# Strassen block products in part of a down projection, a triangular inverse moved to GpSimd, norm sums in three pieces

## The chip, the cores and the metric

The kernel runs on one core of a Trainium2 chip. The metric is the device time of one execution in microseconds (us). Engines are named as in the profile: PE is TensorE's matmul stream, DVE VectorE, ACT ScalarE, POOL GpSimd, SP SyncE, which only issues DMAs here.

## What is computed

One layer of a hybrid decoder on 512 prompt tokens and 8 decode tokens, 520 in all, in fp32, with D = 1024 and a hidden width of 2816:

```python
def swiglu(x, w_gate, w_up, w_down):
    return (jax.nn.silu(x @ w_gate) * (x @ w_up)) @ w_down
...
x = x + 0.5 * rmsnorm(swiglu(rmsnorm(x, ffn1_pre_g), ...), ffn1_post_g)
m, ... = token_mixer(rmsnorm(x, mix_pre_g), ...)
x = x + rmsnorm(m, mix_post_g)
x = x + 0.5 * rmsnorm(swiglu(rmsnorm(x, ffn2_pre_g), ...), ffn2_post_g)
```

The mixer projects with `w_in`, runs four heads of retention (with rope) and four heads of gated DeltaNet side by side, gates and merges both branches and projects with `w_out`. The chunked DeltaNet solves a unit lower triangular system for every chunk of tokens:

```python
a_mat = jnp.eye(c) + jnp.where(strict, bc[..., :, None] * dm * kk, 0.0)
u_v = lax.linalg.triangular_solve(a_mat, bc[..., None] * vc, left_side=True, lower=True, unit_diagonal=True)
```

## The kernel before

**Products.** Features lie on the 128 partitions, tokens along the free axis in two halves of HC = 260. An fp32 product is made of three passes on split operands (`passes`, L294 to L296): high weight by high x, high weight by low x, low weight by high x. One *step* is a contraction tile of 128 for both halves, that is 6 matmuls of 128x260. Weights are split on the chip: ACT copies the high part (L254), DVE subtracts for the low part (`wlo`, L255).

**Stages.** FFN1's gate and up projections run to 245 us of the profiled span, its down projection from there to 378, the mixer to about 870, FFN2's gate and up to 1115 and its down projection to 1247; the last norm and the output follow. Most gate/up tiles are already made by Strassen's scheme: a pair of tiles as seven block products (`seven`, table `SEVEN`) that collect in seven PSUM banks (`sv`), whose weight blocks (L273, 128x512) are summed by adding DMAs and by DVE.

**Down** (L487 to L518) makes 8 output tiles one after another; each has 22 steps over the hidden tiles, in weight units of 8, 7 and 7 contraction tiles. Hidden tiles (`h`) are split into `hh` (ACT, L606) and `hl` (DVE, L608): the first 10 (`SPLIT_H`) while gate/up still runs, the other 12 by the generator `late` when down has begun. When tile 2 begins, the next x is loaded by 8 DMAs of 260 KB.

**Order.** Everything is issued in program order, one in-order queue for each engine. `product`, `seven` and `staged` call `tick()` after each step; side work (hidden tiles, norms, mixer heads) is written as generators that give a number of ticks at each `yield` and are continued when the clock of ticks gets there. So a row on DVE or POOL stands where its tick stands, and a row that waits holds all behind it on its engine. Weights are loaded by SP into two raw buffers (`RAW_BUFS`), split into nine slots (`SPLIT_BUFS`) and looked two units ahead; a pool of 68 slots (`big`) holds x, h, operands and results.

**The inverse** (`inverse`, L1251) of a DeltaNet head: the diagonal blocks of 32 rows are inverted by forward substitution, 31 columns with a multiply (L1279) and a subtract (L1280) each over 128 partitions = 16 blocks by 8 groups of result columns, 4 columns a group. Heads 0 and 2 run on POOL, heads 1 and 3 on DVE. The result goes through DRAM (`s2`, one write of 64 KB at L1283, four reads at L1286) and a transpose on DVE (L1293); then larger blocks are put together on PE (`pV` at L1303 is the first).

**Norm sums.** `sums` (L356, `ss`) adds the squares of 65 tokens at a time over partitions by a matmul with one column, 4 pieces a half (`PIECES`, `PW`); `root` takes the power on POOL (L351, `rs`); `spread` (L362, `rb`) spreads it over the partitions by one matmul a piece.

Of the kernel before, what the change touches and what calls it, by code (L numbers as in the profile page):

```python
# [15 lines left out]
P = 128  # L16
# [15 lines left out]
PIECES, PW = 4, HC // 4  # L32
# [8 lines left out]
SPLIT_H = 10  # L41
# [19 lines left out]
def units():  # L61

    out = []
    for f in (1, 2):
# [4 lines left out]
        for d in range(KD):  # L69
            out += [(f"dn{f}", d, 0, 8), (f"dn{f}", d, 8, 15), (f"dn{f}", d, 15, 22)]  # L70
# [15 lines left out]

SEVEN = ((0, "B11", 0), (2, "T3", 1), (0, "T2", 3), (2, "T4", 4), (1, "B21", 5), (0, "T1", 6), (0, "B22", 9))


def stream(first):  # L90

    at = []
    for m in range(first, KF):
        for i, (_, _, place) in enumerate(SEVEN):
            if m == KF - 1 and i == 4:
                place = 6.5
            at.append((7 * m + place, m, i))
    return [(m, i) for _, m, i in sorted(at)]


class Kernel:
    def __init__(self, ctx, tc, a):
# [14 lines left out]
        for u in self.unit_list:  # L117
            if u[0] != "seven":
# [3 lines left out]
            if u[1:3] not in pairs:  # L122
                g += 1
                pairs[u[1:3]] = g
            self.group.append(pairs[u[1:3]])
# [13 lines left out]
        self.tasks = []  # L139
        self.hold = False  # L140
# [4 lines left out]
    def spawn(self, gen):  # L145
        self.tasks.append([self.now, gen])

    def tick(self):
# [3 lines left out]
        for t in list(self.tasks):  # L152
            if t[0] <= self.now:
                try:
                    t[0] = self.now + (next(t[1]) or 1)
# [32 lines left out]
    def load_to(self, j):  # L188

        nc, a = self.nc, self.a  # L190
        while self.raw_next < min(self.group[min(j, len(self.unit_list))] + RAW_BUFS, self.group[-1]):
            u = self.unit_list[self.first_of[self.raw_next]]
            if u[0] == "seven":
# [10 lines left out]
                t = [t[:, 0:KH], s3, None, a22, t[:, KH:KD], s1, None]  # L204
            else:
# [11 lines left out]
    def cost(self, j):  # L217
        return 1 if self.unit_list[j][0] == "seven" else 2

    def prefetch(self, force=False, most=9):  # L220
# [5 lines left out]
        while self.split_next < min(last, len(self.unit_list)):  # L226
            j = self.split_next
            seven = self.cost(j) == 1
            if seven and self.hold_sums and not force:
                break  # L230
            if j >= self.use_next + (8 if seven and self.ahead else self.ahead) or self.slots_used + self.cost(j) > free:
                break
            if seven:
# [23 lines left out]
    def split_seven(self, j):  # L257
# [16 lines left out]
        if i == 4:  # L274
            t[s4] = self.slot("s4", (P, KH, P))
            nc.vector.tensor_tensor(t[s4], t[4], t[s2], ALU.subtract)

# [76 lines left out]
    def sums(self, ps, acc, n):  # L354
        for c in range(n):
            self.nc.tensor.matmul(ps[0:PW, c : c + 1], acc[:, c * PW : (c + 1) * PW], self.ones[:, 0:1], start=True, stop=True)  # L356

    def spread(self, r):

        pb = self.bank("rb")  # L360
        for c in range(PIECES):
            self.nc.tensor.matmul(  # L362
                pb[:, c * PW : (c + 1) * PW], r[0:PW, c : c + 1].to_broadcast([PW, P]), self.ident[0:PW, 0:PW], start=True, stop=True
# [41 lines left out]
    def pre_rms(self, xs, r, plus):  # L405
# [3 lines left out]
        for hf in range(2):  # L409
            for k in range(KD):  # L410
                while len(xs[hf]) <= k:
                    yield 1
# [3 lines left out]
        while not self.leads:  # L416
            yield 1
# [68 lines left out]
    def down(self, xin, pieces, gpost, gnext, held, plus=None, plus_next=None, x_from=None):  # L486
# [4 lines left out]
        xs, r = [[], []], [None, None]  # L491

        def evac(d, hf, ps):
            if len(y) <= d:
                y.append(self.slot("y"))
            c0, n = HALVES[hf]
            self.square_sum(acc[hf], ps, hf, d == 0, nc.vector)
# [11 lines left out]
        for d in range(KD - held):  # L509
            if d == 2 and x_from is not None:  # L510
                self.x = [self.slot("x") for _ in range(KD)]
                for k in range(KD):
                    nc.sync.dma_start(out=self.x[k], in_=x_from[:, k, :])
            ps = self.product(job(), xin, "dn")
            for hf in range(2):
                evac(d, hf, ps[hf])
        self.staged([job] * held, sum(pieces), xin, "dn", lambda j, hf, ps: evac(KD - held + j, hf, ps), False)
# [33 lines left out]
    def token_factors(self, xs, gcol, F):  # L551

        nc = self.nc
        while len(xs[1]) < KD or not self.rooted:
            yield 1
# [24 lines left out]

    def seven(self, F, name, banks, i):

        b, tokens, _ = SEVEN[i]
# [12 lines left out]
    def ffn(self, plain, xs, r, gpre, gpost, gnext, plus, plus_next, x_from):  # L596
        nc = self.nc
        tt = nc.vector.tensor_tensor
        hx = [[], []]
        hs = []  # L600
        F = {x: [] for x in ("B11", "B21", "B22", "T1", "T2", "T3", "T4")}

        def split_h(h):
# [5 lines left out]
            for hf, (c0, n) in enumerate(HALVES):  # L609
                hx[hf].append((hh[:, c0 : c0 + n], hl[:, c0 : c0 + n]))  # L610

        def hidden(pg, pu):

            h = self.slot("h")
            while r[0] is None or r[1] is None:
                yield 1
# [10 lines left out]
            yield 2  # L627
            yield from split_h(h)

        def pair(m):  # L630
# [39 lines left out]
            def second(t):  # L670
# [5 lines left out]
                if m < SPLIT_H:  # L676
                    yield 1
                    yield from split_h(h)
                else:
                    hs.append(h)  # L680
# [6 lines left out]
        def leads():  # L687
            for j in range(0, len(lead), 2):
                yield from hidden(*lead[j : j + 2])
# [946 lines left out]
```

## Time and profile before

| | |
|---|---|
| median of 3 runs | 1265.9 us (1264.64 to 1267.73) |
| profiled execution | 1265.27 us |
| span in its trace | 1263.5 us |
| PE busy | 1214.7 us (96%) |
| DVE busy | 864.6 us (68%) |
| ACT busy | 538.5 us (43%) |
| POOL busy | 255.9 us (20%) |
| HBM traffic | 131 GB/s over the span |

The shares are means over stages that differ. In the two down stages DVE is busy for less than a third of the time; in gate/up and in parts of the mixer for eight to nine tenths. The table of waits says after which instruction PE went on, and the windows of the trace say for a stretch how busy each engine was and which share of its full clock TensorE was granted.

### The profile page before, as it was taken

Reading aid. Unit: us, or ns where it says so; the run is one execution under the profiler, and the core shown is the slowest. Engines: PE = TensorE matmul, PEld = TensorE weight load, DVE = VectorE, ACT = ScalarE, POOL = GpSimd, SP = SyncE. Lnnn points to the kernel's source line nnn. Section 1 sums busy time; section 2 is a strip of 40 time slices with the busy share of each in tenths; the row PEclk is TensorE's granted clock in tenths of the full one; section 3 lists DMA queues with packets and bytes.
Section 4 is the critical chain, followed back from the end, with each engine's and each line's share of the span. In section 5 each row is a group of like instructions: output and inputs, shape, how many; then the busy total and the mean of one; then the engine's idle time right before and its main releaser. Section 6 shows DMA issues by size and latency. Waiting matters only on the chain.

```text
span 1263.5 us, 25461 instructions
## 1 busy us (share of the span) xinstructions
PE 1214.7 (96%) x10073; PEld 1203.5 (95%) x10073; DVE 864.6 (68%) x1911; ACT 538.5 (43%) x1117; POOL 255.9 (20%) x378
## 2 busy tenths in 40 slices
PE   8999999999999998899999999999989999999995
PEld 7999999999999998899999999999989999999995
DVE  8888888653347887878786766547878878852224
ACT  6566555432234654213334333334645655542210
POOL 4111112000023257136401112204211111100003
PEclk8999999999999899999999999999989999999997
DMA  5677777353332233232434554322377777524321
GB/s 176 178 185 193 184 180 176 94 157 92 91 94 68 87 101 112 77 95 85 129 123 123 197 179 151 118 84 84 122 201 180 178 178 184 144 78 160 92 76 68
DMA packets 76552, 166.60 MB, mean 132 GB/s; under 512 B 14481, under 2 KB 19953, under 8 KB 76433
## 3 DMA queue, kind: packets, MB, share of 16 engines
q1 hardware_dynamic: 64144, 140.69, 34.9%
q0 software_dynamic: 12288, 24.29, 11.3%
q8 instruction: 79, 1.29, 0.4%
q14 instruction: 41, 0.33, 0.1%
HBM read 155.24 MB, written 9.70 MB: 131 GB/s over the span
## 4 chain that ended last, share of the span: by engine, by line
PE 72%; DVE 13%; DMA 4%; issue 3%; ACT 3%; POOL 3%; SPq 0%; DVEq 0%; ACTq 0%; POOLq 0%
PE sv L294 9%; PE sv L295 9%; PE sv L296 9%; PE dn L295 7%; PE dn L294 7%; PE dn L296 7%; PE p L294 5%; PE p L295 5%; PE p L296 5%; DMA s<-gu_in 3%; DVE wlo L255 2%; PE br L294 1%; PE br L295 1%; PE br L296 1%; DVE cv L1049 1%
## 5 line engine op out<-in xcount | busy, mean ns | idle before, releaser
L294 PE MATMUL p<-xhl,whi 128*128 128x260 f32 x784 | 234.5, 299 | 0.0
L295 PE MATMUL p<-xhl,whi 128*128 128x260 f32 x784 | 224.8, 287 | 0.0
L296 PE MATMUL p<-xhl,wlo 128*128 128x260 f32 x784 | 224.4, 286 | 0.0
L295 PE MATMUL dn<-hl,whi 128*128 128x260 f32 x704 | 200.1, 284 | 2.7 <-DVE hl L608 2.7
L294 PE MATMUL dn<-hh,whi 128*128 128x260 f32 x704 | 200.1, 284 | 0.4 <-ACT hh L606 0.4
L296 PE MATMUL dn<-hh,wlo 128*128 128x260 f32 x704 | 199.5, 283 | 0.0
L255 DVE TENSOR_TENSOR wlo<-raw,whi 128x1024 fp32r<-128x1024 f32 (+2 forms) x133 | 156.8, 1192 | 56.9 <-ACT whi L254 56.7
L294 PE MATMUL sv<-th,w 128*128 128x260 f32 x592 | 169.0, 285 | 3.4 <-ACT u L640 3.2
L296 PE MATMUL sv<-th,w 128*128 128x260 f32 x592 | 168.3, 284 | 0.0
L295 PE MATMUL sv<-tl,w 128*128 128x260 f32 x592 | 168.1, 284 | 0.0
L254 ACT CAST whi<-raw 128x1024 fp32r<-128x1024 f32 (+2 forms) x133 | 128.1, 979 | 59.3 <-DMA raw<-dn_in 52.0
L294 PEld LDWEIGHTS p<-xhl,whi 128*128 128x128 f32 x784 | 151.4, 193 | 0.7
L295 PEld LDWEIGHTS p<-xhl,whi 128*128 128x128 f32 x784 | 151.6, 193 | 0.1
L296 PEld LDWEIGHTS p<-xhl,wlo 128*128 128x128 f32 x784 | 151.1, 193 | 0.0
L273 DVE TENSOR_TENSOR w<-s,w 128x512 fp32r<-128x512 f32 x148 | 101.4, 689 | 52.7 <-ACT w L272 51.0
L295 PEld LDWEIGHTS dn<-hl,whi 128*128 128x128 f32 x704 | 133.3, 189 | 3.3 <-DVE hl L608 3.3
L294 PEld LDWEIGHTS dn<-hh,whi 128*128 128x128 f32 x704 | 133.2, 189 | 0.6 <-ACT hh L606 0.6
L296 PEld LDWEIGHTS dn<-hh,wlo 128*128 128x128 f32 x704 | 133.5, 190 | 0.0
L294 PE MATMUL sv<-xhl,w 128*128 128x260 f32 x444 | 126.2, 284 | 5.2 <-DVE t L619 4.6
L215 POOL DMA_DIRECT2D s<-gu_in x74 | 65.0, 977 | 320.1 <-DMA s<-gu_in 152.0
L295 PE MATMUL sv<-xhl,w 128*128 128x260 f32 x444 | 125.7, 283 | 0.0
L296 PE MATMUL sv<-xhl,w 128*128 128x260 f32 x444 | 125.4, 282 | 0.0
(364 smaller groups left out, 2891.6 us busy)
## 6 DMA issues: line engine op xcount, KB each, us to landing
raw<-gu_in SPq DMA_DIRECT2D x50, 512.0 KB, 4.6
raw<-win_in SPq DMA_DIRECT2D x49, 512.0 KB, 3.6
s<-gu_in SPq DMA_DIRECT2D x74, 256.0 KB, 5.3
s<-gu_in POOLq DMA_DIRECT2D x74, 256.0 KB, 4.9
raw<-dn_in SPq DMA_DIRECT2D x32, 448.0 KB, 3.4
a<-gu_in SPq DMA_DIRECT2D x37, 256.0 KB, 5.5
raw<-dn_in SPq DMA_DIRECT2D x16, 512.0 KB, 3.5
x<-x SPq DMA_DIRECT2D x16, 260.0 KB, 5.4
```

Source lines behind the costliest of these rows:

```text
L215: self.nc.gpsimd.dma_start(out=out, in_=term, accum_op=ALU.add)
L254: self.nc.scalar.copy(hi[:, ks], t[:, ks])
L255: self.nc.vector.tensor_tensor(lo[:, ks], t[:, ks], hi[:, ks].bitcast(F32), ALU.subtract)
L273: nc.vector.tensor_tensor(w[:, 1], t[i], w[:, 0].bitcast(F32), ALU.subtract)
L294: mm(ps, hi[:, k, :], xh, start=first, stop=False, skip_group_check=more)
L295: mm(ps, hi[:, k, :], xl, start=False, stop=False, skip_group_check=more)
L296: mm(ps, lo[:, k, :], xh, start=False, stop=last, skip_group_check=more)
L1049: nc.vector.scalar_tensor_tensor(out=acc, in0=cin[:, j : j + SEQ], scalar=w[:, j : j + 1], in1=acc, op0=ALU.mult, op1=ALU.add)
```

## The change

**Down.** Tile 0 and tile 7 stay plain products, with their units in the order 8..14, 15..21, 0..7. Tiles 1 to 6 are made in pairs, three in each FFN. For a pair, contraction tiles 8 to 21 are 14 plain steps for each tile (`rest`); the other 8 are a 2x2 block product (two output tiles by two token halves, contraction in two halves of four tiles), made by seven block products of 4 contraction tiles, 12 matmuls each, of sums of weight blocks and of h blocks. The seven go to six banks, four of which already hold the plain part.

```diff
+DOWN7 = ((0, "B11"), (2, "B21"), (4, "T4"), (0, "N"), (1, "T3"), (0, "T1"), (3, "B22"))
...
-            out += [(f"dn{f}", d, 0, 8), (f"dn{f}", d, 8, 15), (f"dn{f}", d, 15, 22)]
+            rest = [(f"dn{f}", d, 8, 15), (f"dn{f}", d, 15, 22)]
+            if d in (0, KD - 1):
+                out += rest + [(f"dn{f}", d, 0, 8)]
+            else:
+                out += rest
+                if d % 2 == 0:
+                    out += [("down7", f, d - 1, i) for i in range(7)]
...
+    def split_down7(self, j):
+        ...
+        a11, a12, a21, a22 = self.loaded[self.group[j]]
+        if i == 3:
+            tt(a22, a21, a22, ALU.add)
+            tt(a21, a21, a11, ALU.add)
+            tt(a11, a11, a22, ALU.add)
+            tt(a12, a12, a11, ALU.add)
+        src = (a11, a12, a22, a11, a21, a22, a12)[i]
+        w = self.whl.tile([P, 2, KH, P], F32R, tag="w", name=self.name("w7"))
+        ...
+        self.nc.scalar.copy(w[:, 0], src)
+        tt(w[:, 1], src, w[:, 0].bitcast(F32), ALU.subtract)
```

A pair's blocks use two raw loads of 512 KB, both raw buffers, until the last of the seven is split. The results come together on DVE from copies that ACT makes of banks that are used again:

```diff
+    def down_pair(self, rest, F, done, load_x):
+        ...
+        for z in range(2):
+            banks += self.product([(self.next_unit(), range(7)), (self.next_unit(), range(7, 14))], rest, "dn")
+        ...
+        for i in range(7):
+            self.product7(DOWN7, F, "dn", banks, i)
+            if i == 0:
+                v["p"] = self.work("u", HC)
+                nc.scalar.copy(v["p"], banks[a])
+            elif i == 1:
+                add(0, 0, v["p"], banks[r11])
+            elif i == 3:
+                v["u"] = self.work("u", HC)
+                nc.scalar.copy(v["u"], banks[a])
+                if load_x:
+                    load_x()
+            elif i == 4:
+                v["qs"] = self.work("q", HC)
+                nc.scalar.copy(v["qs"], banks[q])
+                v["qu"] = self.work("c", HC)
+                tt(v["qu"], banks[q], v["u"], ALU.subtract)
+                add(1, 0, v["qu"], banks[r21])
+            ...
```

`add` is one DVE addition and then the square, its sum and y, as before. The loads of x move from tile 2 into the third pair, behind its fourth block.

**Hidden tiles.** `SPLIT_H = (8, 21)`: tiles 8 to 20 are split while gate/up runs; tile 21 and tiles 0 to 7 by a generator when down has begun. The latter gives 16 halves of 260 columns and, for four pairs of tiles, four DVE sums of 260 and two splits of 520:

```diff
+        def down_operands():
+            ...
+            for k in range(KD):
+                for hf, (c0, n) in enumerate(HALVES):
+                    first8[hf].append(parts(late[k][:, c0 : c0 + n], "hp"))
+                yield 2
+            for k in range(KH):
+                ...
+                tt(ta[:, 1], x12, x22, ALU.subtract)
+                tt(tb[:, 0], ta[:, 1], x11, ALU.subtract)
+                tt(tb[:, 1], x21, tb[:, 0], ALU.add)
+                tt(ta[:, 0], x11, x12, ALU.subtract)
+                yield 1
+                for t, names in ((tb, ("N", "T4")), (ta, ("T1", "T3"))):
+                    hi, lo = self.slot("th", (P, 2, HC), F32R), self.slot("tl", (P, 2, HC), F32R)
+                    nc.scalar.copy(hi, t)
+                    tt(lo, t, hi.bitcast(F32), ALU.subtract)
```

DVE where the first down tile's results are taken (`y`): before, between the last of the late `hl` and the splits of the next weights:

```order
L608 TENSOR_TENSOR hl_3673<-h_3215,hh_3672 128x520
L608 TENSOR_TENSOR hl_3683<-h_3351,hh_3682 128x520
L498 TENSOR_SCALAR y_3692<-dn_3500,gh 128x260
L498 TENSOR_SCALAR y_3692<-dn_3501,gh 128x260
L255 TENSOR_TENSOR wlo_3698<-raw_3498,whi_3697 128x896
L255 TENSOR_TENSOR wlo_3712<-raw_3576,whi_3711 128x1024
L255 TENSOR_TENSOR wlo_3766<-raw_3701,whi_3765 128x896
```

and now, with the parts of tiles 0 to 7 (`hp`) and the first operand sums (`ta`, `tb`, `tl`) ahead of them:

```order
L840 TENSOR_TENSOR hp_3680<-h_1305,hp_3680 128x260
L840 TENSOR_TENSOR hp_3683<-h_1305,hp_3683 128x260
L861 TENSOR_TENSOR ta_3698<-h_411,h_873 128x260
L862 TENSOR_TENSOR tb_3699<-ta_3698,h_411 128x260
L863 TENSOR_TENSOR tb_3699<-h_873,tb_3699 128x260
L864 TENSOR_TENSOR ta_3698<-h_411 128x260
L869 TENSOR_TENSOR tl_3711<-tb_3699,th_3710 128x520
L608 TENSOR_SCALAR y_3714<-dn_3508,gh 128x260
L608 TENSOR_SCALAR y_3714<-dn_3509,gh 128x260
L302 TENSOR_TENSOR wlo_3720<-raw_3506,whi_3719 128x896
L302 TENSOR_TENSOR wlo_3736<-raw_3582,whi_3735 128x896
```

The first tile's results and the next weights (`wlo`) now stand behind the operand work on DVE.

**Inverse.** All four heads substitute on POOL. The 8 groups now hold columns g, g+8, g+16 and g+24, so that column j touches only the first j//8 + 1 of the four, and the result is written by 8 DMAs:

```diff
-        yield from self.inverse(AT, out, nc.vector if h % 2 else nc.gpsimd)
+        yield from self.inverse(AT, out, nc.gpsimd)
...
-            n = 31 - j
+            n, nq = 31 - j, j // 8 + 1
...
-        nc.sync.dma_start(out=s2.rearrange("b c (g q) i -> (b c g) (q i)", q=4), in_=T.rearrange("p q i -> p (q i)"))
+        columns = s2.rearrange("b c (q g) i -> g (b c) q i", q=4)
+        for g in range(8):
+            nc.sync.dma_start(out=columns[g], in_=T[g:P:8])
```

DVE before, in the substitution of head 1 (`pack` is its work tile, `rp` and `u` are retention's rope, `gdr` the decode norm):

```order
L1279 TENSOR_TENSOR pack_6347<-L_6343,pack_6347 128x4x28
L1280 TENSOR_TENSOR pack_6347<-pack_6347 128x4x28
L1379 COPY gdr_6535<-cb_6587 128x64
L1065 TENSOR_TENSOR rp_6590<-p_6515,cos_5395 128x260
L1066 TENSOR_TENSOR u_6591<-p_6515,sin_5396 64x260
L1067 TENSOR_TENSOR u_6591<-p_6515,sin_5396 64x260
L1068 TENSOR_TENSOR rp_6590<-rp_6590,u_6591 128x260
L1065 TENSOR_TENSOR rp_6590<-p_6516,cos_5395 128x260
```

POOL now, at the same head (L1438 and L1439 are the two lines of the substitution, `rdec` a copy of rope's result for decode):

```order
L1438 TENSOR_TENSOR pack_6488<-L_6484,pack_6488 128x28
L1439 TENSOR_TENSOR pack_6488<-pack_6488 128x28
L1227 COPY rdec<-rp_6738 128x8
L1438 TENSOR_TENSOR pack_6488<-L_6484,pack_6488 128x27
L1439 TENSOR_TENSOR pack_6488<-pack_6488 128x27
L1438 TENSOR_TENSOR pack_6488<-L_6484,pack_6488 128x26
```

The two rows a column have left the queue that carries rope and stand on POOL around a copy that needs rope's result.

SP before, at the end of head 1's substitution, whose result is `pack_6347`:

```order
L1415 DMA sd_7149<-sgdn_in 128x512
L208 DMA raw_7173<-win_in 128x1024
L1283 DMA s_1166_7210<-pack_6347 128x128
L1286 DMA pack_6347<-s_1166_7210 32x4x32 x4
L1415 DMA sd_7256<-sgdn_in 128x512
```

and now, where it is `pack_6488`:

```order
L1576 DMA sd_7297<-sgdn_in 128x512
L251 DMA raw_7321<-win_in 128x1024
L1444 DMA s_1235_7358<-pack_6488 64x1x32 x8
L1447 DMA pack_6488<-s_1235_7358 32x4x32 x4
L1576 DMA sd_7411<-sgdn_in 128x512
```

One write has become eight between a load of decode state or weights (`sd`, `raw`) and the next.

**Norm sums.** `PIECES` goes from 4 to 3 and `PW` from 65 to 87 (three of 87 cover 260 tokens with one taken twice); the power works on 87x6 and 87x3 in place of 65x8 and 65x4.

The other edits (`LATER`, which is empty, the count of spawned generators, `yield 0`) move no instruction.

Over the whole program PE has 9208 matmuls and transposes in place of 9280, of which down has 72 fewer. DVE has 30 instructions more, ACT 86, POOL 124 and SP 28.

## Rows read from the trace of the kernel before

**Rows 1.** Page: busy us (share of the span) and instructions of each engine

```profile
PE 1214.7 (96%) x10073; PEld 1203.5 (95%) x10073; DVE 864.6 (68%) x1911; ACT 538.5 (43%) x1117; POOL 255.9 (20%) x378
```

**Rows 2.** PE's waits by line and releaser: us total, times, longest

```profile
PE sv L294 <- DVE t L619: 4.6, 1, 4.6
...
PE cs L1371 <- DVE gsq L1483: 3.2, 1, 3.2
...
PE dn L295 <- DVE hl L608: 2.7, 3, 1.3
...
PE po L1110 <- DVE st L1118: 2.0, 1, 2.0
PE pV L1303 <- DVE pack L1279: 1.5, 1, 1.5
...
PE ks L1214 <- DVE S L1230: 1.3, 1, 1.3
```

**Rows 3.** Windows: busy us (instructions) by engine, granted clock, DMA share, GB/s

```profile
64.00:96.00 32.00, 32.00 (x271) 32.00 (x270) 28.67 (x56) 20.25 (x43) 5.21 (x6) 1.00 0.76 191
274.00:366.00 92.00, 92.00 (x768) 92.00 (x768) 27.66 (x41) 19.86 (x29) 0.00 (x0) 1.00 0.37 114
...
480.00:512.00 32.00, 28.00 (x219) 27.36 (x217) 26.26 (x74) 10.22 (x28) 21.32 (x48) 0.95 0.35 97
640.00:672.00 32.00, 32.00 (x276) 31.45 (x275) 27.96 (x106) 10.56 (x25) 3.45 (x6) 0.95 0.30 103
1118.00:1130.00 12.00, 10.27 (x71) 9.87 (x71) 9.37 (x14) 8.62 (x16) 0.00 (x0) 0.86 0.46 145
```

**Rows 4.** VectorE's groups by line: busy us, mean ns, idle before, releaser

```profile
L255 DVE TENSOR_TENSOR wlo<-raw,whi 128x1024 fp32r<-128x1024 f32 (+2 forms) x133 | 156.8, 1192 | 56.9 <-ACT whi L254 56.7
L273 DVE TENSOR_TENSOR w<-s,w 128x512 fp32r<-128x512 f32 x148 | 101.4, 689 | 52.7 <-ACT w L272 51.0
...
L608 DVE TENSOR_TENSOR hl<-h,hh 128x520 fp32r<-128x520 f32 x44 | 28.8, 695 | 1.5 <-ACT hh L606 1.5
...
L668 DVE TENSOR_TENSOR h<-c,s 128x260 f32<-128x260 f32 x37 | 15.7, 423 | 0.0
```

**Rows 5.** Groups by line, 458 to 672 us: VectorE, then GpSimd

```profile
L1280 DVE TENSOR_TENSOR pack<-pack 128x124 f32<-128x124 f32 (+30 forms) x62 | 16.0, 258 | 2.1
L1279 DVE TENSOR_TENSOR pack<-L,pack 128x124 f32<-128x124 f32 (+30 forms) x62 | 13.6, 219 | 0.8
...
L1280 POOL TENSOR_TENSOR pack<-pack 128x124 f32<-128x124 f32 (+30 forms) x62 | 23.9, 386 | 4.9
L1279 POOL TENSOR_TENSOR pack<-L,pack 128x124 f32<-128x124 f32 (+30 forms) x62 | 22.8, 368 | 4.0 <-DMA L<-s 0.8
L1069 POOL COPY rdec<-rp 128x8 f32<-128x8 f32 x8 | 8.0, 1005 | 32.0 <-DVE rp L1068 27.7 <-PE sT L1093 4.3
```

**Rows 6.** Line L1279 by engine: ns min/median/max, first and last start us

```profile
L1279 POOL TENSOR_TENSOR pack<-L,pack x62: 196/302/1235, 458.6 to 615.2; 128x124 f32<-128x124 f32 x2, 128x120 f32<-128x120 f32 x2, 128x116 f32<-128x116 f32 x2, 128x112 f32<-128x112 f32 x2
L1279 DVE TENSOR_TENSOR pack<-L,pack x62: 134/218/285, 500.8 to 671.0; 128x124 f32<-128x124 f32 x2, 128x120 f32<-128x120 f32 x2, 128x116 f32<-128x116 f32 x2, 128x112 f32<-128x112 f32 x2
```

**Rows 7.** VectorE in order of time, 627.5 to 630 us: start, us

```profile
628.57 0.28 DVE L1279 TENSOR_TENSOR pack<-L,pack 128x124 f32<-128x124 f32 x1
```

**Rows 8.** GpSimd's groups by shape; PE at a norm: start, us, idle

```profile
L1151 POOL TENSOR_TENSOR rr<-se,mhalf 128x8 f32<-128x8 f32 x4 | 8.5, 2132 | 5.1 <-DVE cin L1038 5.1
...
L351 POOL TENSOR_TENSOR rs<-ms,mhalf 65x8 f32<-65x8 f32 x3 | 6.5, 2162 | 25.1 <-DVE ms L347 25.1
...
378.76 0.63 PE L356 MATMUL ss<-ones,acc 128*65 128x1 f32 x8 [0.92 <-DVE acc L395]
...
382.84 1.10 PE L362 MATMUL rb<-cst,rs 65*128 65x65 f32 x8 [1.19 <-POOL rs L351]
```

**Rows 9.** DMA issues by group: KB each, median us from issue to landing

```profile
x<-x SPq DMA_DIRECT2D x16, 260.0 KB, 5.4
...
s<-pack SPq DMA_DIRECT2D x4, 64.0 KB, 3.2
```

More of the change, by code (lines that the diff above doesn't have):

```diff
@@ L31 @@
 HALVES = ((0, HC), (HC, HC))
-PIECES, PW = 4, HC // 4
+PIECES, PW = 3, -(-HC // 3)
+PIECE_AT = [i * (HC - PW) // (PIECES - 1) for i in range(PIECES)]
 KH = KD // 2
@@ L117, in __init__ @@
         for u in self.unit_list:
-            if u[0] != "seven":
+            if u[0] not in ("seven", "down7"):
                 g += 1
@@ L154, in tick @@
                 try:
-                    t[0] = self.now + (next(t[1]) or 1)
+                    steps = next(t[1])
+                    if steps:
+                        t[3] += 1
+                        steps += t[2].get(t[3], 0)
+                    t[0] = self.now + max(steps, 1)
                 except StopIteration:
@@ L204, in load_to @@
                 t = [t[:, 0:KH], s3, None, a22, t[:, KH:KD], s1, None]
+            elif u[0] == "down7":
+                t = []
+                for d in (u[2], u[2] + 1):
+                    raw = self.raw.tile([P, KD, P], F32, tag="raw", name=self.name("raw"))
+                    nc.sync.dma_start(out=raw, in_=a[f"dn{u[1]}"][d, :, 0:KD, :])
+                    t += [raw[:, 0:KH], raw[:, KH:KD]]
             else:
@@ L688, in leads @@
             for j in range(0, len(lead), 2):
-                yield from hidden(*lead[j : j + 2])
+                yield from hidden(j // 2, *lead[j : j + 2])
         self.spawn(leads())
@@ L701, in ffn @@
             if n == 3:
-                self.spawn(hidden(pg, pu))
+                self.spawn(hidden(plain - 1, pg, pu))
             if m not in pairs:
@@ L705, in ffn, with parts @@
             banks, at = pairs[m]
-            self.seven(F, "sv", banks, i)
+            self.product7(SEVEN, F, "sv", banks, i)
             at(i)
-        def late():
-            while len(hx[1]) < SPLIT_H or len(hs) < KF - SPLIT_H:
-                yield 1
-            for h in hs:
-                yield from split_h(h)
-                yield 1
-        self.spawn(late())
-        return self.down(hx, (8, 7, 7), gpost, gnext, 1, plus, plus_next, x_from)
+        def parts(src, name):
+            t = self.slot(name, (P, 2, HC), F32R)
+            nc.scalar.copy(t[:, 0], src)
+            tt(t[:, 1], src, t[:, 0].bitcast(F32), ALU.subtract)
+            return t[:, 0], t[:, 1]
@@ L720, in run @@
+        self.spawn(down_operands())
+        return self.down(first8, (8, 7, 7), gpost, gnext, 1, plus, plus_next, x_from, (rest, first8, D))
     def run(self):
```

162 lines of the change are left out of this document (117 added, 45 removed).

## The prediction

> **What bounds the kernel now.** I read the busy times first: PE is busy 1214.7 of 1263.5 us, DVE 864.6, POOL 255.9 [rows 1]. PE is the bound, so only two things can shorten the span: less work for PE, and fewer moments in which PE stands still or runs slowly. The table of PE's waits says after whom it stood still [rows 2], and the windows say where another engine is close to full [rows 3]. In the middle of the first down stage PE is busy 92.00 of 92 us with 768 matmuls while DVE is busy 27.66 [rows 3]: there nothing but PE counts, and a matmul of 260 columns costs 92.00/768 = 0.120 us. In the mixer it is otherwise: between 480 and 512 us PE is busy 28.00 of 32, DVE 26.26, POOL 21.32, and the granted clock is 0.95 [rows 3]. The long waits there end with a DVE instruction (`cs` 3.2, `po` 2.0, `pV` 1.5, `ks` 1.3 us, together 8.0 [rows 2]): DVE's queue is in the way. All sums below start from the profiled execution, 1265.3 us (span 1263.5 plus 1.8 around it); the median of the runs is 0.6 us higher.
>
> **Down: PE's share.** A pair's first 8 contraction tiles cost 8 steps x 6 matmuls x 2 tiles = 96 matmuls; seven blocks of 12 cost 84. Six pairs save 6 x 12 = 72 matmuls, 72 x 0.120 = **8.6 us**, all on the path because PE never waits there [rows 3]. The seven use the same 260 columns, so no price by matmul changes.
>
> **Down: what it adds on DVE.** A pair has 4 block sums and 7 splits of 512 columns where two splits of 1024 stood: 11 x 0.69 - 2 x 1.19 = +5.2 us, and six more operations of 260 columns, 6 x 0.42 = +2.5 us [rows 4]. A pair takes PE (168 + 84) x 0.120 = 30 us, and DVE is now busy about 0.30 of such a stretch [rows 3], so it goes from 9 to some 17 us of 30. That is covered. The tight place is the start. From the end of gate/up PE has 22 steps of tile 0, 28 of the first pair and three blocks before the first block that needs in-place sums: 50 x 0.72 + 3 x 1.44 = 40 us. DVE owes until then one `hl` (0.70), 16 parts of 260 (6.8), 16 operand sums (6.8), 8 splits of 520 (5.6), six weight splits (7), two results (1) and 8 operations of 512 (5.5): 33 us of 40. So it fits in sum, but each split stands behind the ACT copy that it subtracts and behind the queue shown in the first piece of order. The last `hl` now has 14 plain steps (10 us) of cover, which had none in the kernel before; against that, tile 0's third unit needs the eight pairs of parts at 0.85 us a step when PE eats 0.72, a lag of 8 x 0.13 = 1 us at most if they start on time. In before the same place cost 2.7 us of waits over both stages [rows 2] and, in the second, a window at clock 0.86, that is 0.14 x 12 = 1.7 us [rows 3]. I take new waits of 1 to 2 us at each start, equal to what they replace: **0**, with -4 (none left) and +6 (3 us more at each start) as ends. Later pairs need two raw loads, both buffers, before the next unit's load can go; those units are used 20 us of PE later. The third pair's x load sets 8 x 260 KB ahead of tile 7's last unit on SP; a load of x lands 5.4 us after its issue in the middle of its burst [rows 9]. I take **+0.5**, with 0 and +3.
>
> **Hidden tiles.** Thirteen instead of ten are split within gate/up. There DVE is at 28.67 of 32 with PE at 32.00 where such splits already stand [rows 3], so they are free. At the start of FFN2's stream, where PE waits 4.6 us for one DVE result [rows 2], the first hidden tiles' splits go from the queue ahead of it, about one 0.70 us operation [rows 4]: **-0.6**, with 0 and -2.
>
> **Substitution.** DVE loses 62 pairs of operations, 16.0 + 13.6 = 29.6 us [rows 5], from the very queue that ends PE's waits. POOL takes them. Its operation costs 0.38 us in the mean against DVE's 0.24 [rows 5], and the smallest 0.196 [rows 6], so the staircase, which halves the elements (1984 to 920 a head for each kind), saves some 0.1 us of each: with a gap of 0.08 an odd head needs 62 x (0.30 to 0.45) = 19 to 28 us of POOL. On DVE head 3 takes from 628.6 to 671.0 [rows 6, 7], 42 us, in which POOL is nearly empty (3.45 of 32 us [rows 3]). So there is room. POOL's own rows there wait mostly for DVE (`rdec` 27.7 us [rows 5]); these waits shrink too. DVE gets 4 to 5 tenths of a microsecond back at each of 62 places, and what PE waits for comes sooner. If all of the four waits went and the two windows at clock 0.95 became full (0.05 x 32 = 1.6 each), this would give 8.0 + 3.2 = 11 us. The `cs` wait alone has a second cause, a power of 2.1 us on POOL behind head 0's substitution [rows 8], which the staircase shortens only in part. Other queues (the rope, the weight splits of 1.19 us) remain, so a wait often comes back smaller elsewhere. I take half: **-6**, with 0 and -11.
>
> The Trainium skill ("GPSIMD Engine Reference", 4.1 Engine selection) speaks against this edit: elementwise work with two inputs is said to be about 2x slower on GpSimd than on VectorE. Here the means are 0.38 and 0.24 us, 1.6x [rows 5], and by 2x an odd head would take 62 x (0.48 + 0.08) = 35 us (an estimate from that page and DVE's row), still under 42.
>
> **The write of s2.** Eight DMAs in place of one occupy SP seven issues longer for each head, and the last lands that much later; before, the write took 3.2 us to land [rows 9]. The cover is 16 ticks (16 x 0.72 = 11.5 us) until the transpose needs the result, and the raw loads queued behind on SP are looked two units (12 us) ahead. I take **0**, up to +2.
>
> **Norm sums.** Eight records of `ss` take 0.63 us and eight of `rb` 1.10 for a half [rows 8]; six take 0.16 less and, if the price is by matmul, 0.27 less (by columns nothing). There are 12 such halves, partly behind other waits. The power at 65x8 takes 2.16 us [rows 8] and gets a quarter fewer columns. I take **-2**, with 0 and -5.
>
> **Sum.** -8.6 + 0 + 0.5 - 0.6 - 6 + 0 - 2 = -16.7: 1265.3 - 16.7 = 1248.6, on the median **1249 us**. All good ends give -8.6 - 4 - 2 - 11 - 5 = -31, all bad ones -8.6 + 6 + 3 + 2 = +2.
>
> **Rivals.** (a) *Only PE's work goes.* The waits in the mixer move instead of going, since the rope and weight splits on DVE stay and PE meets the next row of the same queue. For it: 26.26 of 32 us on DVE hold only some 2 us of substitution in that window, which starts on DVE at 500.8 [rows 3, 6]. Against it: `pV` waits on the substitution itself [rows 2]. It gives 1265.9 - 8.6 - 1 = 1256, half a step up or down for the starts.
>
> (b) *The starts of down eat the gain.* DVE's 33 of 40 us turn out tight because each low part waits for ACT, the first pair's blocks come late, and the clock falls after each wait as it did at 1118 to 1130 [rows 3]. At 3 us of wait and 1.7 of clock beyond the old ones in each stage, 9.4 us, with nothing from the mixer: 1265.9 - 8.6 - 1 + 9.4 = 1266, no change.
>
> (c) *Slower: POOL becomes late.* POOL's queue holds an odd head's 62 operations around `rdec`, powers and the memset before `pV`. One of them took 1.24 us at the longest [rows 6]. Head 3 has 42 us less 4 to 5 of other work, so 38/62 = 0.61 us for each with its gap; beyond that the inverse is late and PE waits at `pV`. At 0.80 that is 62 x 0.19 = 12 us for each odd head, 24 in all: 1265.9 - 8.6 - 1 + 24 = 1280. It decides from 0.69 on, where 2 x 62 x 0.08 = 10 us use up PE's gain. Against it: the median is 0.302 us at the old size [rows 6].
>
> The Trainium skill ("SBUF — State Buffer", Who interferes with whom) names a cause for (c): a DVE instruction with both inputs in SBUF contends with a GpSimd instruction that reads SBUF. The maximum of 1.24 against the median of 0.302 [rows 6] would fit; that most rows are near the median shows that it is not the rule here.
>
> (d) *Everything gives way*: the waits go, and the clock with them: 1265.9 - 26 = 1240.
>
> **Chances.** Forecast (1244 to 1253) 0.45, (a) 0.24, (b) 0.10, (c) 0.09, (d) 0.12. The range reaches from (d) to the poor side of (a): 1239 to 1261. About 0.3% (3.8 us) is what a measurement of this kernel can tell from no change. Faster by more: 0.45 + 0.24 + 0.12 and a little of (b), 0.82; within 0.09; slower 0.09.
>
> **What would show it.** In the profile after: 72 fewer `dn` matmuls at 0.120 us and down shorter by 4 us in each FFN; DVE near 0.55 to 0.6 in the pairs with PE at full share; at the starts, waits of `dn` for `hp`, `tl` or block splits of 1 to 2 us; the substitution only on POOL at about 0.3 us each; `cs`, `po` and `pV` waits for DVE at half of 8.0 us. Wrong would be: a `dn` wait of over 3 us at the first block products, POOL's substitution over 0.6 us, or new waits of the transposes for `s2`.

## The result and the profile after

| | before | after |
|---|---|---|
| median of four runs each | 1266.4 us (1264.6 to 1267.7) | 1252.4 us (1248.9 to 1253.4) |
| ratio, 95% interval | | 0.988 (0.987 to 0.989) |
| profiled execution's span | 1263.5 us | 1247.2 us |

The forecast was 1249 us in a range of 1239 to 1261. The gain is 14 us between the medians and 16.3 between the two profiled executions; the one of after is the fastest of its four. The page's first line of after, which answers to [rows 1]:

```profile
PE 1199.9 (96%) x9953; PEld 1187.0 (95%) x9953; DVE 904.1 (72%) x1941; ACT 570.4 (46%) x1203; POOL 279.5 (22%) x502
```

PE is busy 14.8 us less, DVE 40 us more (904.1 against 864.6), POOL 24 more. The page has 120 PE instructions fewer, 72 of `dn` and 24 each of `ss` and `rb`, and not 72 in all as the section on the change has it. Not all of the 14.8 us is work that is gone: the 72 matmuls are 8.6 us of it, and the mean granted clock rose from 0.977 to 0.982, which over the span makes some 6 us (an estimate from these two figures). What PE waited for in after (engine, line, releaser, us in total, times, longest), which answers to [rows 2]:

```profile
PE sv L359 <- DVE t L751: 5.9, 1, 5.9
...
PE dn L361 <- DVE wlo L302: 2.4, 5, 0.6
...
PE cs L1532 <- DVE gsq L1644: 1.7, 1, 1.7
PE po L1268 <- POOL pack L1438: 1.6, 1, 1.6
PE sp L1589 <- DMA sd<-sret_in: 1.5, 2, 1.3
...
PE dn L359 <- ACT u L571: 0.9, 2, 0.5
PE sp L1589 <- DMA sd<-sgdn_in: 0.8, 1, 0.8
...
PE pV L1464 <- DVE pack L1454: 0.3, 1, 0.3
```

In the mixer `cs` is the norm sum of a head's decode vectors, `po` a product of retention, `ks` one of DeltaNet and `sp` a product with decode state. Of the four waits that ended with DVE and made 8.0 us, `cs` is left with 1.7, and those of `po` and `ks` for DVE and of `pV` for DVE's substitution are gone; `pV` waits 0.3 us for the transpose. `po` waits 1.6 us for POOL's substitution (`pack`), where 0.9 us stood for POOL before, and new are 2.3 us of `sp`, in two rows, for the load of that state. In down the wait for `hl` is gone and smaller ones for `wlo` and for ACT's copy `u` have come. The windows (busy us and count by engine, granted clock, DMA share, GB/s), which answer to [rows 3], with the first pair in FFN1's down as the second row:

```profile
274.00:366.00 92.00, 90.64 (x750) 89.98 (x749) 57.70 (x105) 35.11 (x64) 0.00 (x0) 1.00 0.37 114
259.00:300.00 41.00, 40.42 (x334) 39.98 (x333) 31.74 (x66) 17.68 (x37) 0.00 (x0) 1.00 0.23 71
640.00:672.00 32.00, 32.00 (x272) 31.47 (x271) 20.09 (x58) 9.74 (x23) 10.89 (x28) 1.00 0.38 114
```

From 274 to 366 us PE was busy 92.00 us before and is 90.64 now, DVE 27.66 before and 57.70 now; in the first pair DVE is at 31.74 of 41, which is more than the 0.55 to 0.6 that the prediction named for the pairs. In the mixer the window of 640, whose clock was 0.95, is at 1.00 with DVE at 20.09 instead of 27.96. The same view over the whole mixer, from the first `p` to the first `br`, before and then after:

```profile
375.40:682.80 307.40, 292.99 (x2464) 287.67 (x2463) 246.29 (x719) 119.56 (x280) 118.71 (x214) 0.97 0.33 101
```

```profile
373.80:672.40 298.60, 288.19 (x2452) 282.74 (x2451) 220.50 (x595) 119.85 (x281) 143.96 (x338) 0.98 0.34 103
```

PE stands still 10.4 us there instead of 14.4, so 4 of the 8.9 us are shorter waits. The other 4.8 are busy time, with all but 12 of the instructions the same: they ran at a higher granted clock, 0.98 in the mean instead of 0.97.

The stages tell where the time went. Each is measured on PE's instructions: from the first matmul of one kind to the first of the next (gate/up, `dn`, `p`, `br`, gate/up, `dn`, the last `ss`). The kernels in the lower rows are those of the experiments. Each row is one profiled execution, which can lie several us off its kernel's median (down alone: 1264.8 against 1258.6).

| us | gate/up 1 | down 1 | mixer, `p` to `br` | branches to FFN2 | gate/up 2 | down 2 | rest |
|---|---|---|---|---|---|---|---|
| before | 240.6 | 130.1 | 307.4 | 186.6 | 245.5 | 133.5 | 15.1 |
| after | 243.1 | 126.2 | 298.5 | 186.2 | 245.2 | 129.0 | 14.5 |
| down alone | 244.7 | 126.2 | 308.7 | 186.6 | 249.0 | 128.2 | 14.8 |
| inverse alone | 240.6 | 130.4 | 301.4 | 186.5 | 245.8 | 132.3 | 14.8 |
| three pieces alone | 242.0 | 130.1 | 307.8 | 186.3 | 248.2 | 131.7 | 14.8 |
| odd heads on DVE | 245.8 | 126.3 | 303.5 | 186.4 | 243.7 | 127.4 | 14.5 |
| no staircase, one write | 243.6 | 126.1 | 301.5 | 186.4 | 245.3 | 129.0 | 14.5 |
| no staircase, eight writes | 244.2 | 126.0 | 304.7 | 186.2 | 249.6 | 127.3 | 15.1 |
| after again | 245.1 | 125.9 | 299.0 | 186.2 | 247.6 | 127.3 | 14.4 |
| four writes | 240.1 | 125.8 | 296.4 | 186.3 | 247.0 | 127.4 | 14.5 |
| four writes again | 241.4 | 126.1 | 295.2 | 186.3 | 245.6 | 128.5 | 14.5 |
| x later | 242.6 | 126.1 | 294.4 | 186.3 | 248.4 | 127.5 | 14.4 |
| more splits late | 243.0 | 132.6 | 299.1 | 186.0 | 248.1 | 135.7 | 15.1 |

Read down a column: down and the mixer repeat to 1 or 2 us among kernels that agree there, while the two gate/up stages scatter over 6 us (240.1 to 245.8, 243.7 to 249.6) in kernels that agree there. Whether the three more hidden tiles that are split there are free is not shown: the first gate/up stage has a mean of 241.1 us in the three kernels with ten such tiles and 243.4 in the nine with thirteen, but 243.0 with six (the last row). So a whole run is uncertain by some microseconds through gate/up, and what an edit does in its own stage is read better from the stage.

### The profile page after: what moved, and what is told of

Same layout as the page of the kernel before. It is cut to its first block, busy times and chain, and to the rows that moved or that the text cites. A ratio compares the mean times of both kernels' runs of the same rounds, so it can differ in the third digit from the quotient of the medians.

```text
span 1247.2 us, 25546 instructions
## 1 busy us (share of the span) xinstructions
PE 1199.9 (96%) x9953; PEld 1187.0 (95%) x9953; DVE 904.1 (72%) x1941; ACT 570.4 (46%) x1203; POOL 279.5 (22%) x502
## 4 chain that ended last, share of the span: by engine, by line
PE 66%; DVE 15%; DMA 7%; ACT 6%; issue 3%; POOL 2%; SPq 1%; ACTq 0%; DVEq 0%; POOLq 0%
PE sv L359 9%; PE sv L361 8%; PE sv L360 8%; PE p L359 6%; PE p L360 5%; PE p L361 5%; PE dn L361 5%; PE dn L359 5%; PE dn L360 5%; DMA s<-gu_in 4%; DVE wlo L302 3%; DMA raw<-dn_in 2%; ACT whi L301 1%; PE br L359 1%; PE br L360 1%
## 5 line engine op out<-in xcount | busy, mean ns | idle before, releaser
L302 DVE TENSOR_TENSOR wlo<-raw,whi 128x1024 fp32r<-128x1024 f32 (+2 forms) x121 | 142.6, 1184 | 40.7 <-ACT whi L301 38.9
L359 PEld LDWEIGHTS p<-xhl,whi 128*128 128x128 f32 x784 | 149.7, 191 | 0.7
L360 PEld LDWEIGHTS p<-xhl,whi 128*128 128x128 f32 x784 | 149.9, 191 | 0.1
L359 PE MATMUL sv<-xhl,w 128*128 128x260 f32 x444 | 126.3, 284 | 6.5 <-DVE t L751 5.9
L361 PE MATMUL dn<-hh,wlo 128*128 128x260 f32 x448 | 127.1, 284 | 1.9 <-DVE wlo L302 1.9
L301 ACT CAST whi<-raw 128x1024 fp32r<-128x1024 f32 (+2 forms) x121 | 116.5, 971 | 26.1 <-DMA raw<-dn_in 18.4
L359 PE MATMUL dn<-hh,whi 128*128 128x260 f32 x448 | 127.2, 284 | 0.1
L360 PE MATMUL dn<-hl,whi 128*128 128x260 f32 x448 | 126.6, 283 | 0.0
L361 PE MATMUL sv<-xhl,w 128*128 128x260 f32 x444 | 125.9, 283 | 0.0
L319 ACT CAST w<-s 128x512 fp32r<-128x512 f32 x148 | 91.4, 619 | 62.8 <-DVE s L315 32.8
L359 PEld LDWEIGHTS sv<-th,w 128*128 128x128 f32 x592 | 112.3, 190 | 5.2 <-ACT u L771 4.9
L360 PEld LDWEIGHTS sv<-tl,w 128*128 128x128 f32 x592 | 112.3, 190 | 0.0
```

The costliest lines, as they stand in the source:

```text
L301: self.nc.scalar.copy(hi[:, ks], t[:, ks])
L302: self.nc.vector.tensor_tensor(lo[:, ks], t[:, ks], hi[:, ks].bitcast(F32), ALU.subtract)
L319: nc.scalar.copy(w[:, 0], t[i])
L359: mm(ps, hi[:, k, :], xh, start=first, stop=False, skip_group_check=more)
L360: mm(ps, hi[:, k, :], xl, start=False, stop=False, skip_group_check=more)
L361: mm(ps, lo[:, k, :], xh, start=False, stop=last, skip_group_check=more)
```

## Experiments

**Each part by itself.** Three kernels take one part of the change each: the block products in down with `SPLIT_H`, the inverse, the three pieces.

The first has down as changed, and the rest put back:

```diff
-PIECES, PW = 3, -(-HC // 3)
+PIECES, PW = 4, HC // 4
...
-        yield from self.inverse(AT, out, nc.gpsimd)
+        yield from self.inverse(AT, out, nc.vector if h % 2 else nc.gpsimd)
```

(with the old layout and its one write in `inverse`).

> The kernel before with the block products in down alone (inverse and norm sums as before). My theory: 72 matmuls fewer and starts that wait no longer than before, 7 to 9 us less than before, about 1258; the waits of the mixer for VectorE (cs, po, pV, ks, 8.0 us) stay. Rival, that the starts of down eat the gain: 1262 or more. Rival, that the mixer's shorter time is a shift of phase that any change ahead of it would bring: 1252 to 1254, the mixer about 9 us shorter here too.

Measured: 1258.6 against 1266.9 us of the kernel before on that chip, ratio 0.994 (0.992 to 0.996), 8.3 us less. Down is 3.9 and 5.3 us shorter, the mixer is not (308.7). Its waits for DVE, from the table of PE's waits, are those of before:

```profile
PE cs L1529 <- DVE gsq L1641: 3.5, 1, 3.5
...
PE po L1268 <- DVE st L1276: 2.0, 1, 2.0
```

So the mixer's gain does not come from a mere shift of what lies ahead of it; as the whole cause that rival is out.

The second has the inverse alone:

```diff
-        yield from self.inverse(AT, out, nc.vector if h % 2 else nc.gpsimd)
+        yield from self.inverse(AT, out, nc.gpsimd)
...
-            n = 31 - j
+            n, nq = 31 - j, j // 8 + 1
...
+        for g in range(8):
+            nc.sync.dma_start(out=columns[g], in_=T[g:P:8])
```

> The kernel before with the inverse's change alone: all four heads on GpSimd, staircase, eight writes. My theory: 7 to 10 us less than before, 1256 to 1259, all of it in the mixer, with the waits of sp for decode state (about 2 us) that the eight writes bring. Rival, phase: 0 to 3 us less.

Measured: 1258.3 us, ratio 0.993 (0.991 to 0.995), 8.6 us less than the same runs of before; the mixer is 6.0 us shorter, so the profile does not show all of it in the mixer, as was expected. The waits of PE that matter:

```profile
PE sp L1431 <- DMA sd<-sret_in: 2.0, 1, 2.0
...
PE sp L1431 <- DMA sd<-sgdn_in: 1.4, 1, 1.4
```

The loads of decode state (`sd`) are waited for here too, 3.4 us. The mixer of the whole change is 8.9 us shorter, 3 more than here, while down alone (308.7) and the pieces alone (307.8) make it no shorter. What lies ahead of the mixer may thus move the size of its gain by some 3 us; no run settles it.

The third has the pieces alone:

```diff
-PIECES, PW = 4, HC // 4
+PIECES, PW = 3, -(-HC // 3)
+PIECE_AT = [i * (HC - PW) // (PIECES - 1) for i in range(PIECES)]
```

> The kernel before with the norm sums in three pieces alone. My prediction's term: 2 us less, 1264. The trace after puts the waits for the power at 2.2 in place of 2.5 us and the ss and rb records at about the same, by which it would be 0 to 1 us, no difference that this measurement tells.

Measured: 1266.2 us, ratio 0.9996 (0.998 to 1.002). No difference that can be told. PE's wait for the power, 2.5 us in all before, reads here:

```profile
PE rb L364 <- POOL rs L352: 2.2, 2, 1.2
```

The three make 8.3 + 8.6 + 0.7 = 17.6 us, against 14.0 for the whole change in its first runs and 16.5 in the repeat below.

**What in the inverse does it.** Two things were changed at once: who substitutes, and how many elements a step has. First the odd heads go back to DVE, with staircase and eight writes kept:

```diff
-        yield from self.inverse(AT, out, nc.gpsimd)
+        yield from self.inverse(AT, out, nc.vector if h % 2 else nc.gpsimd)
```

> The changed kernel with heads 1 and 3 back on VectorE, the staircase and the eight writes kept. My theory, that what counts is VectorE's queue: most of the mixer's gain goes, 1256 to 1260, and the waits for VectorE (po, pV, ks) come back. Rival, that the staircase is what shortens the mixer, whoever runs it: 1251 to 1254.

Measured: 1257.4 us, ratio 0.992 (0.989 to 0.995), as my theory had it. The mixer takes 303.5, so 5.0 us of its 8.9 go, little more than half. The waits for DVE and for the memset (`TT`) behind the substitution on POOL are back, while `cs` stays small:

```profile
PE po L1268 <- POOL TT L1449: 2.5, 1, 2.5
...
PE cs L1532 <- DVE gsq L1644: 1.6, 1, 1.6
...
PE pV L1464 <- DVE pack L1438: 1.3, 1, 1.3
```

Then the old layout with all four heads on GpSimd:

```diff
-            n, nq = 31 - j, j // 8 + 1
+            n = 31 - j
...
-        for g in range(8):
-            nc.sync.dma_start(out=columns[g], in_=T[g:P:8])
+        nc.sync.dma_start(out=s2.rearrange("b c (g q) i -> (b c g) (q i)", q=4), in_=T.rearrange("p q i -> p (q i)"))
```

> The changed kernel with all four heads on GpSimd but the old layout: all four column groups in every step, one write. In the profiles so far the stretch from the first w_in product to the first branch product took 307.4 us before, 298.5 after, 303.5 with the odd heads on VectorE and the staircase. If relief of VectorE and shorter substitution each give their part and add, this stretch is about 302 to 303 here, the whole 1255 to 1257. If the eight writes cost what their waits show (sp for decode state, 2.3 us after), these waits are gone and it is 300 to 301. If the relief of VectorE is all, 299.

and the same with eight writes:

```diff
-        nc.sync.dma_start(out=s2.rearrange("b c (g q) i -> (b c g) (q i)", q=4), in_=T.rearrange("p q i -> p (q i)"))
+        columns = s2.rearrange("b c (g q) i -> g (b c) q i", q=4)
+        for g in range(8):
+            nc.sync.dma_start(out=columns[g], in_=T[g:P:8])
```

> The same with the old layout written by eight DMAs in place of one; nothing else differs. If the issue time on SP (5.0 us for eight in place of 0.44) delays the loads of decode state behind it, sp waits of about 2 us come back and the mixer is 1 to 3 us longer than with one write. If these loads have slack, no difference.

Measured: 1252.1 us (ratio 0.987, 0.985 to 0.990) with one write and 1257.6 (0.992, 0.989 to 0.994) with eight; the mixer takes 301.5 and 304.7. With one write the whole is below the 1255 to 1257 expected and the stretch between the two expected values. The waits in the mixer (420 to 690 us) with one write, then with eight:

```profile
PE cs L1529 <- DVE gsq L1641: 5.2, 1, 5.2
...
PE pV L1461 <- DVE pack L1451: 1.4, 2, 1.2
```

```profile
PE cs L1531 <- DVE gsq L1643: 5.1, 1, 5.1
PE sp L1588 <- DMA sd<-sret_in: 2.4, 2, 2.1
...
PE sp L1588 <- DMA sd<-sgdn_in: 0.7, 1, 0.7
```

SP's rows show the reason (start, us, engine, line, operation). With one write, after head 2's substitution:

```profile
609.46 0.44 SPq L1441 DMA_DIRECT2D s<-pack  x1
...
615.41 0.43 SPq L1573 DMA_DIRECT2D sd<-sgdn_in  x1
618.32 0.33 SPq L251 DMA_DIRECT2D raw<-win_in  x1
618.69 0.92 SPq L1573 DMA_DIRECT2D sd<-sret_in  x2
```

With eight:

```profile
610.57 4.92 SPq L1443 DMA_DIRECT2D s<-pack  x8
...
619.03 0.43 SPq L1575 DMA_DIRECT2D sd<-sgdn_in  x1
619.50 0.44 SPq L251 DMA_DIRECT2D raw<-win_in  x1
619.99 0.96 SPq L1575 DMA_DIRECT2D sd<-sret_in  x2
```

Eight issues hold SP for 4.92 us where one took 0.44. Behind one write a load of decode state (`sd`, 256 KB) goes 6.0 us after the write began, and the next weights (`raw`, 512 KB) and two more loads of state some 3 us after that; behind eight, the same loads go 8.5 to 9.5 us after it, all within one microsecond. PE's longest wait, 2.1 us, is for one of the last two (`sret_in`): its issue comes hardly later, 9.4 us after the write began instead of 9.2, but it lands 7.65 us after its issue instead of 4.85. Over all 32 loads of state, from issue to landing, one write and then eight:

```profile
DMA to landing us min/median/max: 2.8/4.1/5.6
```

```profile
DMA to landing us min/median/max: 3.4/4.3/7.8
```

At this place, then, the time goes less because the issues hold SP than because the loads behind them go together and take longer to land. In all PE waits 3.1 us for `sd`, of which no row stands with one write; 0.7 of it is behind head 1's write and 0.3 ahead of the one shown.

Step by step the mixer takes 307.4 us before, 301.5 with all heads on GpSimd (6 less), 304.7 with eight writes (3 more) and 298.7 with the staircase, the mean of the two profiles of after (6 less). Seen from after, the move to GpSimd is worth 303.5 - 298.7 = 5. `cs`, 5.1 us without the staircase and 1.7 and 1.5 with it, is over half of what the staircase gives. Whole runs tell less: the old layout with one write (1252.1) and the staircase with eight (1252.1, below) come out alike.

**Fewer writes.** With the staircase's layout, the eight partition groups hold for a column group q the columns 8q to 8q + 7, which lie side by side in `s2`; so four writes of all 128 partitions do:

```diff
-        columns = s2.rearrange("b c (q g) i -> g (b c) q i", q=4)
-        for g in range(8):
-            nc.sync.dma_start(out=columns[g], in_=T[g:P:8])
+        rows = s2.rearrange("b c (q g) i -> q (b c) (g i)", q=4)
+        for q in range(4):
+            nc.sync.dma_start(out=rows[q], in_=T[:, q, :])
```

> The changed kernel with the staircase's result written by four DMAs (one for each column group, all 128 partitions) in place of eight. If SP's issue time is what makes sp wait for decode state, about half of the 2.3 us goes and the whole is 1 to 2 us shorter, 1250 to 1251; otherwise 1252.

> The changed kernel as it is, beside the three others on one chip: 1252, with the stretch of the mixer at 298 to 300 us. The first gate/up stage, whose code the change leaves alone but for the hidden tiles' splits, took 240.5 to 245.8 us in the profiles so far, of kernels with and without the change; if that is chance, it is anywhere in this span here.

Measured side by side: 1248.1 us with four writes (ratio to before 0.985, 0.982 to 0.988), 1252.1 with eight (0.985 to 0.990). The two intervals overlap; the mixer, 296.4 against 299.0, tells more clearly, and no wait for `sd` is left in it. The first row is of PE's waits, the others of SP:

```profile
PE sp L1589 <- DVE st L1276: 0.5, 1, 0.5
```

```profile
601.36 2.50 SPq L1444 DMA_DIRECT2D s<-pack  x4
...
608.14 0.43 SPq L1576 DMA_DIRECT2D sd<-sgdn_in  x1
```

Four issues take 2.50 us, and the first load of state goes 6.8 us after they began, apart again from the later ones (8.9 and 9.3 us).

Once more beside the next two kernels:

> The kernel with four writes again, beside the two others on one chip: 1248 to 1250, the stretch of the mixer at 296 to 298 us.

Measured: 1246.9 us, ratio 0.985 (0.982 to 0.988), mixer 295.2, with 0.8 us of waits for `sd`. By the medians and by the mixer this is faster than both kernels of the case; more went than the half of the 2.3 us that was expected.

**The starts of down and tile 7.** The loads of x are moved behind the pair's last block:

```diff
             elif i == 3:
                 v["u"] = self.work("u", HC)
                 nc.scalar.copy(v["u"], banks[a])
-                if load_x:
-                    load_x()
...
             elif i == 6:
                 add(0, 1, v["v"], banks[r12])
+                if load_x:
+                    load_x()
```

> The kernel with four writes, and the loads of x moved from behind the fourth to behind the seventh block of the third pair. In the changed kernel SP stands 8 us at these loads, waiting for slots, with the last weight load of tile 7 behind them, and PE waits 0.9 us for that unit's low part in each FFN. If that is the cause, both waits go or shrink, 1 to 2 us less than with four writes. Rival: the loads then fall together with the last weights and come too late for the norm; the same or 1 to 2 us more.

Measured: 1247.0 us beside 1246.9 for four writes alone. The waits for `wlo` do not shrink (0.9 us in FFN1), although SP now has all of tile 7's weights ahead of x:

```profile
344.17 9.32 SPq L251 DMA_DIRECT2D raw<-dn_in  x3
...
358.85 3.98 SPq L622 DMA_DIRECT2D x<-xT_in  x8
```

DVE and then ACT show what holds the split (the row at 357.35 is the unit that PE waits for from 357.9 on; its load had landed at 348.7, and in the profile of after, where the same unit is waited for, at 349.3):

```profile
357.35 1.09 DVE L302 TENSOR_TENSOR wlo<-raw,whi 128x896 fp32r<-128x896 f32 x1
```

```profile
356.07 0.42 ACT L460 ACTIVATE s<-t 128x260 f32<-128x260 f32 x1 [1.35 <-DVE t L564]
356.40 0.93 ACT L301 CAST whi<-raw 128x896 fp32r<-128x896 f32 x1
```

The low part goes as soon as ACT has copied the high part, and that copy stands behind the square `s` of an output tile, for which ACT waits until PE's blocks and DVE's sums are done. It is the order on DVE and ACT, not the load; the expectation's cause was wrong.

Last, more hidden tiles are split late:

```diff
-SPLIT_H = (8, 21)
+SPLIT_H = (8, 14)
```

> The changed kernel with hidden tiles 14 to 21, not 21 alone, split after down has begun: seven more low parts of 0.70 us, 4.9 us, on VectorE in each start, in front of the parts and operand sums. My prediction gave VectorE 33 us of work in the 40 that PE takes; if some 5 us of slack are there, PE waits 1 to 3 us more at each start, in all 2 to 5 us, 1254 to 1257. If the start is at its limit already, each start is 5 us longer and the clock falls after it, 1262 or more. If VectorE's work there is free, no change.

Measured: 1263.1 us, ratio to before 0.998 (0.996 to 1.000), against 1252 for the changed kernel: the two down stages are 6.4 and 7 to 8 us longer than after, and with them most of the change's gain is gone. The waits in FFN1's down and the window at its start:

```profile
PE dn L359 <- ACT hh L738: 2.1, 1, 2.1
PE dn L360 <- DVE hl L740: 1.6, 2, 1.2
PE dn L359 <- ACT u L571: 1.5, 1, 1.5
```

```profile
250.00:262.00 12.00, 8.30 (x55) 7.59 (x54) 9.74 (x16) 10.14 (x22) 0.00 (x0) 0.86 0.49 145
```

ACT is busy 10.14 of 12 us there and the granted clock is 0.86 in the mean, after the waits. 4.9 us more of late work on DVE came with 5.2 us of waits, and the clock on top. Of the 5.2 us 3.6 end with ACT, which makes the high parts and which the prediction's sum of 33 us for DVE leaves out. The start has next to no slack for splits that come ahead of their steps.

## Why the prediction was right, point by point

**PE's share, 8.6 us: right.** Down alone gave 8.3 us in the runs, 3.9 and 5.3 by its stages. Over the table's rows, the last one left out, the mean of the first down stage is 4.1 us shorter with the block products than without and that of the second 4.5, together 8.6.

**The starts, 0: right in the sum, the places differ.** In FFN1 the `hl` waits (1.3 us) have no row any more; instead PE waits 0.5 for ACT's copy of a bank that the next block writes again, and 0.9 for tile 7's weights. The new waits of 1 to 2 us foreseen for `hp` and for the first blocks at their sums did not come. The 33 of 40 us were read as slack; more late splits show that slack in a sum over DVE alone is not slack in the queues of DVE and ACT.

**x loads, +0.5: not seen.** With the loads of x moved behind the weights the time is the same (1247.0 and 1246.9 us), though half a microsecond could not be told. The 0.9 us that PE waits at tile 7 look like this term and come from the order of DVE and ACT (above).

**Hidden tiles, -0.6: not there.** The wait at the start of FFN2's stream was 4.6 us in the profile of before and 5.4 to 6.8 in the twelve others, with that edit and without it (5.7 and 6.8). In the trace of after DVE idles 8.8 us ahead of it, until ACT's copy of a weight block whose terms come by adding DMAs: the wait belongs to those loads. The removed split stood behind them in the queue, and one profile's 4.6 was one draw of a scattered value.

**Substitution, -6: the sum near, its division wrong.** The stretch lost 8.9 us in the profiles, about half of it waits and half the clock. I credited DVE's relief and gave the staircase little. The runs give the relief 5 to 6 us, the staircase 6, and charge 3 for the writes. The step that failed is "which the staircase shortens only in part". The power `rr` on POOL reads before, with all heads on POOL and the old layout, and after:

```profile
493.04 2.62 POOL L1151 TENSOR_TENSOR rr<-se,mhalf 128x8 f32<-128x8 f32 x1
```

```profile
492.06 2.61 POOL L1309 TENSOR_TENSOR rr<-se,mhalf 128x8 f32<-128x8 f32 x1
```

```profile
489.08 1.65 POOL L1309 TENSOR_TENSOR rr<-se,mhalf 128x8 f32<-128x8 f32 x1
```

and what waits for it on DVE in after:

```profile
490.76 0.16 DVE L1318 TENSOR_TENSOR cols<-se,rr 128x4 f32<-128x4 f32 x1 [1.73 <-POOL rr L1309]
...
493.78 0.23 DVE L1644 TENSOR_TENSOR gsq<-dcv 128x64 f32<-128x64 f32 x1 [0.41 <-ACT dcv L1641]
```

DVE waits for `rr`, and everything up to `gsq`, for which PE waits at `cs`, follows it by 3 us. It begins at 489.08 us in after and at 493.04 before, 4.0 us sooner, while head 0's substitution begins 0.9 us sooner (457.7 and 458.6): the other 3.1 us are the shorter operations ahead of it on POOL. With the old layout it stays at 492.06. A further 1.0 us is its own length, 1.65 instead of 2.62; that is not the staircase's doing, for the repeat of after has 2.62 as well. So a rather long queue on an engine that is 20% busy over the span set PE's longest wait in the mixer. The operations came out as estimated:

```profile
L1439 POOL TENSOR_TENSOR pack<-pack 128x24 f32<-128x24 f32 (+23 forms) x124 | 38.2, 308 | 9.7
L1438 POOL TENSOR_TENSOR pack<-L,pack 128x24 f32<-128x24 f32 (+23 forms) x124 | 35.9, 290 | 8.8 <-DMA L<-s 1.8
```

0.29 and 0.31 us each, with a gap of some 0.08, against the 0.30 to 0.45 with the gap that was taken from the smallest and the old mean, far from the 0.69 at which rival (c) was to begin to decide. The Trainium skill ("GPSIMD Engine Reference", 4.1 Engine selection) with its factor of two is right on the single operation in its direction and not in its size: with the staircase on both engines the medians of the two lines are 0.243 and 0.252 us on GpSimd and 0.182 and 0.191 on VectorE, 1.3 times as long. It did not decide, since GpSimd had the room.

**The write of s2, 0 to +2: mis-sized.** It cost 3.2 us of mixer. The queue was named, but only the weight loads and the transpose were asked for their slack; the loads of decode state stand there too, and have none. An issue of these writes took some 0.59 us, 4.9 to 5.0 for eight, where the one write took 0.44.

**Norm sums, -2: not seen.** The runs give 0.7 us less, in an interval from 3 us less to 2 more, so -2 is not refuted. What the traces show is 0.3 us less of waiting for the power. That the fewer matmuls lie where PE waits for the norm's chain on DVE anyway would explain it and is not shown.

**Rivals.** (a) is refused by the inverse alone (8.6 us by itself), (c) by the operation times. (b)'s mechanism is real, as the later splits showed, and the change avoids it by splitting thirteen tiles ahead of time. (d) did not come: waits of 5.9 us are left in the rows of the mixer above. Of the signs of being wrong none came: no `dn` wait is over 0.6 us, the substitution takes 0.3 us an operation, and no transpose waits for `s2`.

## What to carry to other kernels

When an engine is the bound, look for its waits in the queue of a lightly used engine too: a slow operation behind many small ones there can set the longest wait, and making the small ones smaller pays as much as moving them. When one DMA becomes eight, count the issue time on the queue and ask every load behind it for its slack, decode state as well as weights, and whether the loads will now go all at once. And compare stages, not only whole runs, when another stage scatters by more than the edit is worth.

## What the runs showed of the hardware

Some of POOL's small operations take four to five times as long as the rest. Two views of after side by side, POOL and then DVE (start, us, engine, line, operation):

```profile
650.95 1.32 POOL L1438 TENSOR_TENSOR pack<-L,pack 128x28 f32<-128x28 f32 x1
652.35 0.25 POOL L1439 TENSOR_TENSOR pack<-pack 128x28 f32<-128x28 f32 x1
```

```profile
650.97 1.21 DVE L302 TENSOR_TENSOR wlo<-raw,whi 128x1024 fp32r<-128x1024 f32 x1
```

The operation of 1.32 us starts with DVE's `wlo` and ends within 0.1 us of it; the next one, with as many elements, takes 0.25. In the profile of after 16 of the 248 operations of the substitution took over 0.6 us, and each of the 16 overlaps a `wlo` or another long DVE instruction with both operands in SBUF. Of 21 operations that overlap `sg`, which reads its product from PSUM, 18 ran at their usual length (0.20 to 0.27 us); the other three met a `wlo` as well. The Trainium skill says so ("SBUF — State Buffer", Who interferes with whom): a DVE instruction with two SBUF inputs contends with a GpSimd instruction that reads SBUF. The trace agrees; the prediction's remark that it is not the rule here holds by number and not by kind. Against the usual 0.245 us the 16 cost POOL 12 us over four heads; those ahead of `rr` delay what PE waits for at `cs`. No run took the cause away, so this is shown by coincidence in time, not by an experiment.
